# Hybrid layer on one core: split weights made three products ahead, and an index search that pauses for the sums of h

## The chip, the cores and the metric

The kernel runs on 1 core of one Trainium2 chip. The metric is device time in microseconds (us): 1913.03 us, median of 3 runs. The core has a matrix engine (TensorE, PE in the profile; its weight loads are the rows PEld), VectorE (DVE), ScalarE (ACT), GpSimd (POOL), and SyncE (SP), which here issues the DMA transfers. Every engine works through its own instructions in the order of the program; they meet through semaphores.

## The reference, cut to what matters

One decoder layer over 1024 tokens and 1024 channels, batch 1, all float32:

```
h    = rmsnorm(x) * (1 + scale1) + shift1            # from the conditioning c
proj = h @ w_in                                      # 1024 x 7240
qa, ka, va, iq, ik, iw, qr, kr, vr, gr, ga, gb = split(proj)
score = sum over index heads of iw * relu(iq . ik)   # causal; keep the 256 largest of a row
att  = softmax attention of qa, ka, va over the kept keys
ret  = chunkwise retention of qr, kr, vr
y    = sigmoid(ga) * (att @ w_attn_proj) + sigmoid(gb) * ((silu(gr) * groupnorm(ret)) @ w_ret_proj)
x    = x + gate1 * (y @ w_out)
x    = x + gate2 * ((silu(h2 @ w_ffn_gate) * (h2 @ w_ffn_up)) @ w_ffn_down)     # h2: second norm of x
out  = rmsnorm(x)
```

## The kernel before

A float32 product is made of three matmuls on values split in two: `hi` (rounded) and `lo = x - hi`, as hi·hi, hi·lo and lo·hi. A weight is split by ACT (`split_block` L703, tile `whi`) and then by POOL (L704, tile `wlo`).

The columns gr, qa, ka, two blocks of gb, and ga, and later the two input matrices of the feed-forward, use Strassen's scheme in Winograd's form on 2 x 2 blocks: seven products (M1 to M7) in place of eight. One `Stream` makes 256 output channels for all 1024 tokens: it loads two raw blocks of weights (`open`, L717), forms the weight side of each product (`factor`: DVE subtractions L732 and L728 for M5, M6, M7 and M4, the plain block for M1, M2 and M3), splits it, and multiplies (`product`, L760, L762 and L764: 12 matmuls of 128x128 by 128x512). M1, M6, M7 and M4 add up in one PSUM bank (`mm`), M5 and M3 in another (`lg`), and M2 has one of its own. ACT copies partial results out of PSUM (L743), DVE adds to them (L746), and `use` finishes each of the four output blocks. The order of products is M1, M5, M6, M3, M7, M2, M4; output 12 is complete after M3, 22 after M7, 11 after M2, 21 after M4.

There are 13 streams in the gate stage, counted from 0: 0 to 3 gr (silu), 4 and 5 qa, 6 and 7 ka, 8 gb, 9 to 12 ga. For the four q and k streams `use` does more: it splits the finished output block like a weight (again L703 and L704, here `whi<-kept`, `whi<-sums` or `whi<-spare`) and stores it with six DMAs (L829, L831). The streams 0 and 1 are interleaved product by product, as are the last two.

The other side of a product is a split part of h, or one of four sums of parts (S1, S2, S4, S3: adds L588 and L590 and the `lo` of L596 on DVE, the `hi` of L595 on ACT), made just before stream 0 needs them. S1 serves M5, S2 M6, S4 M3, and S3 M7.

The index search (`select_all`) finds the 256th largest score of each row bit by bit: for every bit from 30 to 0, six counts on DVE (L449, one for each block of rows) and two small updates (L454, L467; L470 at bit 0), then one more pass of counts and a tail of 30 instructions (L475 to L479). It has a low priority, and a scheduler puts it between other DVE work. Attention, which starts at about 960 us, needs its result.

A scheduler sets the order on every engine from the order of the code, the priorities and its own estimate of times. The code calls `product` for one product after the other, and each call makes its own split weight first.

Of the kernel before, what the change touches and what calls it, by code (L numbers as in the profile page):

```python
# [19 lines left out]
P = 128  # L20
# [4 lines left out]
H = 512  # L25
# [18 lines left out]
def tile_hybrid_layer(ctx: ExitStack, tc: tile.TileContext, x, c, w_ada, b_ada, norm1_w, w_in,  # L44
# [20 lines left out]
    def f32(ap):  # L65
        return ap.bitcast(F32)
# [367 lines left out]
    def select_all():  # L434

        tc.cur_priority += LATE
        n = len(score)  # L440
        cand, rej = (early.tile([P, 8], I32, name=x)[:, :n] for x in ("cand", "rej"))
        cnt, need = (early.tile([P, 8], F32, name=x)[:, :n] for x in ("cnt", "need"))
        eq = early.tile([P, S], U8, name="eq")
        rank = early.tile([P, S], I16, name="rank")
        at = [cand.bitcast(F32)[:, j:j + 1] for j in range(n)]

        def count(op, thr):
            for j, sc in enumerate(score):
                ins = nc.vector.tensor_scalar(eq[:, :sc.shape[1]], sc, thr[j], None, op0=op, op1=ALU.add,  # L449
                                              accum_out=cnt[:, j:j + 1])  # L450
            return ins

        def rejected(value):
            nc.vector.tensor_scalar(rej, cnt, float(TOPK), float(value), op0=ALU.is_lt, op1=ALU.mult)  # L454


        for j, sc in enumerate(score):
            ins = nc.vector.tensor_scalar(eq[:, :sc.shape[1]], sc, 0.0, None, op0=ALU.is_ge, op1=ALU.add,
                                          accum_out=cnt[:, j:j + 1])
            tc.add_manual_dep(ins.ins, last_score[0].ins.name, NOSYNC, reason="scores first")  # L460
        rejected(-1)
        nc.vector.tensor_scalar(cand, rej, 1 << 30, None, op0=ALU.bitwise_xor)
        for bit in range(30, -1, -1):
            count(ALU.is_ge, at)
            rejected(1 << bit)
            if bit:
                nc.vector.scalar_tensor_tensor(cand, cand, 1 << (bit - 1), rej, op0=ALU.bitwise_xor,  # L467
                                               op1=ALU.bitwise_xor)
            else:
                nc.vector.tensor_tensor(cand, cand, rej, op=ALU.bitwise_xor)  # L470
        count(ALU.is_gt, at)
        nc.vector.tensor_scalar(need, cnt, -1.0, float(TOPK), op0=ALU.mult, op1=ALU.add)
        for j, sc in enumerate(score):
            e, r = eq[:, :sc.shape[1]], rank[:, :sc.shape[1]]
            nc.vector.tensor_scalar(e, sc, at[j], None, op0=ALU.is_equal)  # L475
# [3 lines left out]
            nc.vector.scalar_tensor_tensor(sc, e, NEG, sc, op0=ALU.mult, op1=ALU.add)  # L479
        tc.cur_priority -= LATE  # L480
# [112 lines left out]
    def split_sum(to, k, src):  # L593
        hi, lo = (x[:, k, :] for x in side[to])
        nc.scalar.activation(hi, src, AF.Copy)  # L595
        nc.vector.tensor_sub(lo, src, f32(hi))  # L596

    mgen = mod_work()
    for hp in range(2):
# [106 lines left out]
    class Stream:  # L706


        def __init__(self, env, w, c0):
            self.env, self.w, self.c0 = env, w, c0  # L710
            self.c, self.ready = {}, {}

        def open(self):
            self.blocks = {}
            for kh in range(2):
                raw = self.env.raw().rearrange("p (k n) -> p k n", k=4)
                nc.sync.dma_start(out=raw, in_=self.w[kh * H:(kh + 1) * H, self.c0:self.c0 + 2 * P]  # L717
                                  .rearrange("(k p) n -> p k n", p=P))
# [28 lines left out]

        def product(self, m, after=None):

            early = m in self.ready  # L750
            whi, wlo = self.ready[m] if early else self.factor(m)
            hhi, hlo = self.env.side[SIDE[m]]
            if m == "M1":
                self.A = self.env.a()
# [20 lines left out]
                self.add("12", ps)  # L775
            if m == "M7":
                self.add("22", ps)
            if m == "M2" and early and self.env.late_m2:
# [8 lines left out]
    def ring_pair():  # L787
        return tuple(ring.tile([P, H], R, name=n, tag=n, bufs=RING) for n in ("whi", "wlo"))

    class GateEnv:  # L790
        late_m2 = False
        n_q, n_raw = 0, 0

        def __init__(self):
# [13 lines left out]
        def quad(self, *_):  # L808
            self.n_q += 1
            return quads[(self.n_q - 1) % len(quads)]  # L810

        def use(self, st, c):
            src = st.A if c == "21" else st.c[c]
            to = self.quad() if c == "21" else src
            hf, nt = int(c[0]) - 1, int(c[1]) - 1
            cs = slice(hf * H, (hf + 1) * H)
            if st.func is not None:
                nc.scalar.activation(to, src, st.func)
                nc.sync.dma_start(out=st.dst[nt][:, cs], in_=to)
                return  # L820

            if c == "21":
                nc.scalar.activation(to, src, AF.Copy)
            parts = ring_pair()
            split_block(to, *parts)
            which, dst = st.dst
            for e in range(2):
                h = 2 * (st.nt + nt) + e
                nc.sync.dma_start(out=rot_d[:, which, h, :, cs], in_=to[64 * e:64 * e + 16])  # L829
                for i, part in enumerate(parts):  # L830
                    nc.sync.dma_start(out=dst[h, 16:64, i, cs], in_=f32(part[64 * e + 16:64 * e + 64]))  # L831

# [32 lines left out]
    for to, terms in (("S1", [("h12", 1), ("h22", 1)]), ("S2", [(None, 1), ("h11", -1)]),  # L865
                      ("S4", [(None, -1), ("h21", 1)]), ("S3", [("h11", 1), ("h12", -1)])):
        for k in range(4):
            add_up(sums[k], [(n, k, sign) for n, sign in terms])
            split_sum(to, k, sums[k])
    for m in ORDER:  # L870
        for st in flow[:2]:
            st.product(m)


    def rope_load(hf):
# [37 lines left out]
        nc.scalar.activation(hi, sg, AF.Copy)  # L913
        nc.vector.tensor_sub(gT.lo[hf][:, k, :], sg, f32(hi))

    flow[2].open()
    rope = {}
    for n in range(2, len(flow) - 2):
        flow[n + 1].open()
        for m in ORDER:  # L920
            flow[n].product(m)
# [5 lines left out]
    flow[-1].open()  # L927
    for m in EARLY:
        for st in flow[-2:]:
            st.product(m)  # L930
    gT.alloc(0)
    k = 0
    staged = {}
    for m in ("M5", "M6", "M7", "M4", "M3"):
        if m == "M3":
            gT.alloc(1)
        for st in flow[-2:]:
            st.product(m)
            if k < KT:
                make_g(k, 0, *g_load(k, 0, *(f32(x) for x in ring_pair())))  # L940
            k += 1
        if m in ("M5", "M6"):
            stage = sp.tile([P, 8, H], F32, name="stage", tag={"M5": "S1", "M6": "S2"}[m])
            for i in range(4):
                staged[len(staged)] = g_load(len(staged), 1, stage[:, 2 * i, :], stage[:, 2 * i + 1, :])


    stacks = {}
# [344 lines left out]
        return ffn.tile([P, H], F32, name="tmp", tag="tmp", bufs=4)  # L1293

    class FfnEnv:
        late_m2 = True
# [98 lines left out]
    for p in range(NP):  # L1395
        for u, w in enumerate((w_ffn_gate, w_ffn_up)):
            st = streams[p, u] = Stream(fenv, w, 2 * p * P)
            st.p, st.u = p, u
            st.ready = {m: early_w[p, u, m] for m in EARLY if (p, u, m) in early_w}
    turns = {(0, 0, "M1"): {0: 6}, (0, 1, "M1"): {2: 7}}  # L1400
    for p in range(2):
        for m in EARLY:
# [18 lines left out]
    for m in ORDER:  # L1421
        if m not in EARLY:
            for st in flow[:2]:
                st.product(m)
                if m == "M4":
                    fenv.use(st, "11")
    for n in range(2, len(flow)):
        st = flow[n]
        if n == 2:
            st.open()  # L1430
        if n + 1 < len(flow):
            flow[n + 1].open()
        for m in ORDER:
            if st.p > 1 or m not in EARLY:
                st.product(m)
                if m == "M4" and st.p == 1:
                    fenv.use(st, "11")
                for task in todo[:2]:
                    task()
                del todo[:2]  # L1440
    def drain_todo():
        for task in todo:
            task()
# [180 lines left out]
```

## Time and profile before

| | |
|---|---|
| median of 3 runs (1912.8 to 1917.15) | 1913.03 us |
| the profiled execution, its own time | 1912.54 us |
| its span, first to last instruction | 1910.8 us |
| PE busy | 1749.4 us, 92% |
| DVE / POOL / ACT busy | 1210.5 / 930.6 / 741.3 us |
| mean granted PE clock | 0.958 |
| gate stage, first to last product | 499 to 874 us |
| feed-forward, products of gate and up | some 1250 to 1690 us |

The profiled execution stands 0.5 us below the median of the runs. A row of the timeline reads: start, duration, engine, source line, operation, output<-inputs, shapes, count, and in brackets the engine's idle time before it and what ended it. A row of a window reads: stretch, its length, then for each engine the busy time and (number of instructions), the granted PE clock (1.00 is full), the DMA engines' share, GB/s. A row of the waits reads: who waited for whom, us in total, times, longest. A busy PE is not PE at full pace: a matmul that runs at half the clock counts as busy.

### The profile page before, as it was taken

The numbers are of one execution on the slowest core, as the hardware profiler recorded it, in microseconds if no ns is written. First come the engines' busy times: TensorE is split into PE (matmuls) and PEld (weight loads), VectorE is DVE, ScalarE is ACT, GpSimd is POOL, SyncE is SP. The second block draws the span as 40 slices with busy tenths as digits, with TensorE's granted clock in tenths as the row PEclk, the third lists the DMA queues.
The fourth block names the chain that finished last, engine by engine and source line by source line (L and its number), as shares of the span: only waits on it lengthen the run. The fifth ranks groups of instructions, "written<-read, shape, count | busy, mean of one in ns | idle before, by whom it ended". The sixth has DMA issues, their size and how long they took to land. (4 is left out here: it accounts for less than half of the span.)

```text
span 1910.8 us, 24627 instructions
## 1 busy us (share of the span) xinstructions
PE 1749.4 (92%) x8266; PEld 1418.9 (74%) x8266; DVE 1210.5 (63%) x2088; ACT 741.3 (39%) x1448; POOL 930.6 (49%) x902
## 2 busy tenths in 40 slices
PE   5899999999888676999989999979998999999998
PEld 4788768787766454778867788858776788888887
DVE  7637699998999511544156564685666554567465
ACT  3426533323442112443057624553332333355444
POOL 4561393855541333953045462455444544466464
PEclk9999999999998667999999999989999999999999
DMA  8430353425321222577494361023676533277653
GB/s 287 144 89 26 108 150 132 155 53 155 91 94 59 61 81 71 168 243 211 148 205 116 122 232 44 22 77 100 230 254 215 171 105 99 83 242 245 197 171 121
DMA packets 184703, 266.49 MB, mean 139 GB/s; under 512 B 13872, under 2 KB 113664, under 8 KB 182144
## 3 DMA queue, kind: packets, MB, share of 16 engines
q1 hardware_dynamic: 184576, 264.91, 44.3%
q8 instruction: 65, 1.06, 0.2%
q14 instruction: 62, 0.51, 0.1%
HBM read 195.39 MB, written 69.47 MB: 139 GB/s over the span
## 5 line engine op out<-in xcount | busy, mean ns | idle before, releaser
L704 POOL TENSOR_TENSOR flo<-tmp,fhi 128x512 fp32r<-128x512 f32 x88 | 131.1, 1491 | 152.5 <-ACT fhi L703 130.7
L78 POOL TENSOR_TENSOR wlo<-wraw,whi 128x512 fp32r<-128x512 f32 (+2 forms) x116 | 142.9, 1245 | 101.1 <-ACT whi L77 96.0
L449 DVE TENSOR_SCALAR_CACHE_REDUCE eq<-score,cand 128x384 uint8<-128x384 f32 (+2 forms) x192 | 180.5, 940 | 3.6
L116 PE MATMUL mm<-whi,hT_hi 128*128 128x512 f32 (+1 forms) x432 | 162.6, 379 | 2.3 <-ACT qk L608 1.8
L119 PE MATMUL mm<-whi,hT_lo 128*128 128x512 f32 (+1 forms) x432 | 163.0, 379 | 0.0
L118 PE MATMUL mm<-wlo,hT_hi 128*128 128x512 f32 (+1 forms) x432 | 162.6, 377 | 0.0
L760 PE MATMUL ya<-hc,fhi 128*128 128x512 f32 x336 | 133.7, 399 | 13.5 <-DVE c L746 11.7
L762 PE MATMUL ya<-hc,fhi 128*128 128x512 f32 x336 | 132.7, 395 | 5.2 <-DVE hc L1390 5.2
L1472 DVE TENSOR_TENSOR dslot<-draw,dslot 128x512 fp32r<-128x512 f32 x88 | 92.2, 1075 | 70.3 <-ACT dslot L1471 64.1
L764 PE MATMUL ya<-hc,flo 128*128 128x512 f32 x336 | 131.2, 394 | 0.0
L1471 ACT ACTIVATE dslot<-draw 128x512 fp32r<-128x512 f32 x154 | 90.3, 626 | 97.5 <-PE ya L1490 36.2
L1472 POOL TENSOR_TENSOR dslot<-draw,dslot 128x512 fp32r<-128x512 f32 x66 | 97.4, 1485 | 62.1 <-ACT dslot L1471 61.8
L77 ACT ACTIVATE whi<-wraw 128x512 fp32r<-128x512 f32 (+2 forms) x116 | 67.0, 590 | 135.5 <-DMA wraw<-in_w_in_dram 55.8
L704 POOL TENSOR_TENSOR flo<-raws,fhi 128x512 fp32r<-128x512 f32 x58 | 81.6, 1408 | 72.1 <-ACT fhi L703 55.3
L760 PE MATMUL yb<-hc,fhi 128*128 128x512 f32 x248 | 98.0, 395 | 5.2 <-ACT hc L1389 3.7
L703 ACT ACTIVATE fhi<-tmp 128x512 fp32r<-128x512 f32 x88 | 55.3, 631 | 116.7 <-PE ya L762 71.7
L764 PE MATMUL yb<-hc,flo 128*128 128x512 f32 x248 | 96.8, 391 | 3.7 <-POOL flo L704 3.7
L762 PE MATMUL yb<-hc,fhi 128*128 128x512 f32 x248 | 96.8, 390 | 1.8 <-DVE hc L1390 1.7
L704 POOL TENSOR_TENSOR wlo<-wraw,whi 128x512 fp32r<-128x512 f32 x52 | 74.9, 1449 | 44.0 <-ACT whi L703 26.5
L1035 POOL TENSOR_SCALAR sx<-sx,mx 128x1024 f32<-128x1024 f32 (+7 forms) x64 | 47.6, 751 | 97.5 <-DVE mx L1034 72.4
L760 PE MATMUL mm<-hT_hi,whi 128*128 128x512 f32 x156 | 70.1, 453 | 26.4 <-ACT whi L703 25.4
L116 PEld LDWEIGHTS mm<-whi,hT_hi 128*128 128x128 f32 x432 | 82.1, 190 | 14.1 <-ACT qk L608 2.2
(400 smaller groups left out, 5016.3 us busy)
## 6 DMA issues: line engine op xcount, KB each, us to landing
draw<-act_d SPq DMA_DIRECT2D x77, 256.0 KB
mw<-in_w_ada_dram SPq DMA_DIRECT2D x32, 512.0 KB
act_d<-c SPq DMA_DIRECT2D x62, 256.0 KB
raw<-in_w_in_dram SPq DMA_DIRECT2D x26, 512.0 KB
raws<-in_w_ffn_gate_dram SPq DMA_DIRECT2D x24, 512.0 KB
raws<-in_w_ffn_up_dram SPq DMA_DIRECT2D x24, 512.0 KB
dw<-in_w_ffn_down_dram SPq DMA_DIRECT2D x22, 512.0 KB
dw_d<-dw SPq DMA_DIRECT2D x11, 1024.0 KB
```

The source lines that it names most:

```text
L77: nc.scalar.activation(hi[:, :n], raw[:, :n], AF.Copy)
L78: nc.gpsimd.tensor_sub(lo[:, :n], raw[:, :n], f32(hi[:, :n]))
L116: ins = nc.tensor.matmul(ps, lhsT=ahi, rhs=whi[:, :n], start=(i == 0), stop=False)
L118: nc.tensor.matmul(ps, lhsT=ahi, rhs=wlo[:, :n], start=False, stop=False)
L119: nc.tensor.matmul(ps, lhsT=alo, rhs=whi[:, :n], start=False, stop=(i == last))
L449: ins = nc.vector.tensor_scalar(eq[:, :sc.shape[1]], sc, thr[j], None, op0=op, op1=ALU.add, accum_out=cnt[:, j:j + 1])
L704: nc.gpsimd.tensor_sub(lo, src, f32(hi))
L760: mm = nc.tensor.matmul(ps, lhsT=whi[:, k, :], rhs=hhi[:, k, :], start=first, stop=False, skip_group_check=True)
L762: nc.tensor.matmul(ps, lhsT=whi[:, k, :], rhs=hlo[:, k, :], start=False, stop=False, skip_group_check=True)
L764: nc.tensor.matmul(ps, lhsT=wlo[:, k, :], rhs=hhi[:, k, :], start=False, stop=last, skip_group_check=True)
L1471: nc.scalar.activation(slot[:, 0], raw, AF.Copy)
L1472: lo_eng.tensor_sub(slot[:, 1], raw, f32(slot[:, 0]))
```

## The change

A `run` loop takes the list of products in their order and makes the split weight of a later product (three ahead in the gate stage, two in the feed-forward) before it calls `product` for the present one. `open` may now be called by `prepare`. A stream's output stores stay behind the loads of the next stream's raw weights in the DMA queue. The first count of bit 8 of the index search is put behind the last split of S3. Nothing is computed that was not computed before; the number of instructions on each engine is the same.

```diff
+    PAUSE = 8
+    paused = []
...
         for bit in range(30, -1, -1):
-            count(ALU.is_ge, at)
+            first = count(ALU.is_ge, at)
+            if bit == PAUSE:
+                paused.append(first)
...
+        def prepare(self, m):
+            if m not in self.ready:
+                self.open()
+                self.ready[m] = self.factor(m)
...
         def product(self, m, after=None):
-            early = m in self.ready
-            whi, wlo = self.ready[m] if early else self.factor(m)
+            self.prepare(m)
+            whi, wlo = self.ready[m]
...
+    def run(seq, ahead, then=lambda i: None):
+        for st, m in seq[:ahead]:
+            st.prepare(m)
+        for i, (st, m) in enumerate(seq):
+            if i + ahead < len(seq):
+                nxt, nm = seq[i + ahead]
+                nxt.prepare(nm)
+            st.product(m)
+            then(i)
...
+        def store(self, st, dst, src):
+            ins = nc.sync.dma_start(out=dst, in_=src)
+            if st.next:
+                turns_after(ins, st.next.loaded)
...
-            split_sum(to, k, sums[k])
-    for m in ORDER:
-        for st in flow[:2]:
-            st.product(m)
+            split = split_sum(to, k, sums[k])
+    turns_after(paused[0], split)
...
+    seq = [(st, m) for m in ORDER for st in flow[:2]]
+    seq += [(st, m) for st in flow[2:-2] for m in ORDER]
+    n_mid = len(seq)
+    seq += [(st, m) for m in ("M1", "M2", "M5", "M6", "M7", "M4", "M3") for st in flow[-2:]]
...
+    run(seq, 3, behind)
...
+    seq = [(st, m) for m in ORDER if m not in EARLY for st in flow[:2]]
+    seq += [(st, m) for st in flow[2:] for m in ORDER if not (st.early and m in EARLY)]
...
+    run(seq, 2, behind)
```

Lines move a little: L703 is L706 in the changed kernel, L743 L754, L746 L757, L823 L850, L728 L739, L732 L743, L449 L450, L596 L599.

Three places show what the scheduler makes of it. The first is ACT from the copy of output 21 of one q stream (`kept<-mm`, L823) into the next one; `whi<-raw` and `whi<-wraw` are weights, `whi<-kept` and `whi<-spare` split output blocks. Before:

```order
L823 ACTIVATE kept<-mm 128x512
L703 ACTIVATE whi<-kept 128x512
L703 ACTIVATE whi<-raw_4910 128x512
L703 ACTIVATE whi<-wraw 128x512 x2
L703 ACTIVATE whi<-raw_4907 128x512
L743 ACTIVATE kept<-mm 128x512
L743 ACTIVATE kept<-lg 128x512
L743 ACTIVATE spare<-mm 128x512
L703 ACTIVATE whi<-spare 128x512
L703 ACTIVATE whi<-wraw 128x512
L703 ACTIVATE whi<-kept 128x512
L703 ACTIVATE whi<-raw_4907 128x512
```

Behind the split of output 21 stand the weights of M1, M5, M6 and M3, and then, one behind each later output block, those of M7, M2, M4 and the next stream's M1. The same place in the changed kernel:

```order
L850 ACTIVATE kept<-mm 128x512
L706 ACTIVATE whi<-kept 128x512
L706 ACTIVATE whi<-raw_4907 128x512
L706 ACTIVATE whi<-wraw 128x512
L706 ACTIVATE whi<-raw_4907 128x512
L754 ACTIVATE kept<-lg 128x512
L706 ACTIVATE whi<-wraw 128x512
L754 ACTIVATE spare<-mm 128x512
L706 ACTIVATE whi<-spare 128x512
L706 ACTIVATE whi<-raw_4908 128x512
L706 ACTIVATE whi<-kept 128x512
L706 ACTIVATE whi<-wraw 128x512
```

Behind output 21 now stand M3, M7 and M2 and then M4; behind output 12 (`spare`) stands M1 of the next stream, three products on. POOL's order moves in the same way.

The second place is DVE at the end of the sums; `hT_lo` is the `lo` half of S3, which takes the place of a part of h, and the rows `eq,cnt` are counts of the search. Before:

```order
L596 TENSOR_TENSOR hT_lo_122<-sums,hT_hi_121 128x512
L449 TENSOR_SCALAR eq,cnt<-score_769,cand 128x512
L596 TENSOR_TENSOR hT_lo_122<-sums,hT_hi_121 128x512
L732 TENSOR_TENSOR wraw<-raw_4908 128x512
L449 TENSOR_SCALAR eq,cnt<-score_770,cand 128x640
L728 TENSOR_TENSOR wraw<-raw_4907,wraw 128x512
L746 TENSOR_TENSOR sums<-sums,lg 128x512
L449 TENSOR_SCALAR eq,cnt<-score_771,cand 128x768
```

After:

```order
L599 TENSOR_TENSOR hT_lo_122<-sums,hT_hi_121 128x512
L743 TENSOR_TENSOR wraw<-raw_4907,wraw 128x512
L757 TENSOR_TENSOR kept<-kept,lg 128x512
L599 TENSOR_TENSOR hT_lo_122<-sums,hT_hi_121 128x512
L450 TENSOR_SCALAR eq,cnt<-score_768,cand 128x384
L450 TENSOR_SCALAR eq,cnt<-score_769,cand 128x512
L450 TENSOR_SCALAR eq,cnt<-score_770,cand 128x640
L450 TENSOR_SCALAR eq,cnt<-score_771,cand 128x768
```

No count stands among the sums any more; the counts in the first list are those of bit 4, the first after S3 in the second list those of bit 8. From there on DVE has the same work of the streams as before, with the last nine bits and the tail between it: the tail ends after the 21st add of the streams (the last add of stream 6), where it ended after the 15th (the last of stream 4).

The third place is the feed-forward. There no row moves: from the first instruction of attention to the end the order on PE, DVE, ACT, POOL and SP is, line numbers apart, the same before and after.

More of the change, by code (lines that the diff above doesn't have):

```diff
@@ L447, in count @@
         def count(op, thr):
[L448 to L451, printed above, removed]
+            ins = [nc.vector.tensor_scalar(eq[:, :sc.shape[1]], sc, thr[j], None, op0=op, op1=ALU.add,
+                                           accum_out=cnt[:, j:j + 1]) for j, sc in enumerate(score)]
+            return ins[0]
         def rejected(value):
@@ L595, in split_sum @@
         nc.scalar.activation(hi, src, AF.Copy)
-        nc.vector.tensor_sub(lo, src, f32(hi))
+        return nc.vector.tensor_sub(lo, src, f32(hi))
     mgen = mod_work()
@@ L710, in __init__ @@
             self.env, self.w, self.c0 = env, w, c0
-            self.c, self.ready = {}, {}
+            self.c, self.ready, self.blocks = {}, {}, {}
+            self.early = False
+            self.next = None
         def open(self):
-            self.blocks = {}
+            if self.blocks:
+                return
             for kh in range(2):
                 raw = self.env.raw().rearrange("p (k n) -> p k n", k=4)
-                nc.sync.dma_start(out=raw, in_=self.w[kh * H:(kh + 1) * H, self.c0:self.c0 + 2 * P]
-                                  .rearrange("(k p) n -> p k n", p=P))
+                self.loaded = nc.sync.dma_start(out=raw, in_=self.w[kh * H:(kh + 1) * H, self.c0:self.c0 + 2 * P]
+                                                .rearrange("(k p) n -> p k n", p=P))
                 for f in range(2):
                     self.blocks[f"{kh + 1}{f + 1}"] = raw[:, :, f * P:(f + 1) * P]
+        def prepare(self, m):
+            if m not in self.ready:
+                self.open()
+                self.ready[m] = self.factor(m)
         def factor(self, m):
@@ L818, in use @@
                 nc.scalar.activation(to, src, st.func)
-                nc.sync.dma_start(out=st.dst[nt][:, cs], in_=to)
+                self.store(st, st.dst[nt][:, cs], to)
                 return
@@ L828, in use @@
                 h = 2 * (st.nt + nt) + e
-                nc.sync.dma_start(out=rot_d[:, which, h, :, cs], in_=to[64 * e:64 * e + 16])
+                self.store(st, rot_d[:, which, h, :, cs], to[64 * e:64 * e + 16])
                 for i, part in enumerate(parts):
@@ L914, in make_g, with behind @@
         nc.vector.tensor_sub(gT.lo[hf][:, k, :], sg, f32(hi))
[L916 to L921, printed above, removed]
+    seq = [(st, m) for m in ORDER for st in flow[:2]]
+    seq += [(st, m) for st in flow[2:-2] for m in ORDER]
+    n_mid = len(seq)
+    seq += [(st, m) for m in ("M1", "M2", "M5", "M6", "M7", "M4", "M3") for st in flow[-2:]]
+    rope, staged = {}, {}
+    def behind(i):
+        n, m = 2 + (i - 14) // 7, seq[i][1]
+        if 14 <= i < n_mid:
+            if m == "M1":
+                flow[n + 1].open()
+                flow[n].next = flow[n + 1]
             if n in (8, 9) and m == "M1":
@@ L925, in tile_hybrid_layer @@
                 rope_store(n - 9, *rope[n - 9])
[L927 to L935, printed above, removed]
-            gT.alloc(1)
[L937 to L945, printed above, removed]
+        if i == n_mid:
+            flow[-1].open()
+        k = i - n_mid - 4
+        if k == -1:
+            gT.alloc(0)
+        if 0 <= k < KT:
+            make_g(k, 0, *g_load(k, 0, *(f32(x) for x in ring_pair())))
+            if k in (1, 3):
+                stage = sp.tile([P, 8, H], F32, name="stage", tag=f"S{(k + 1) // 2}")
+                for i in range(4):
+                    staged[len(staged)] = g_load(len(staged), 1, stage[:, 2 * i, :], stage[:, 2 * i + 1, :])
+        if k == KT - 1:
+            gT.alloc(1)
+    run(seq, 3, behind)
     stacks = {}
@@ L1420, in tile_hybrid_layer, with behind @@
     flow[1].open()
[L1421 to L1431, printed above, removed]
-            flow[n + 1].open()
[L1433 to L1440, printed above, removed]
+    seq = [(st, m) for m in ORDER if m not in EARLY for st in flow[:2]]
+    seq += [(st, m) for st in flow[2:] for m in ORDER if not (st.early and m in EARLY)]
+    def behind(i):
+        st, m = seq[i]
+        if st.early and m == "M4":
+            fenv.use(st, "11")
+        if i < 10:
+            return
+        n = flow.index(st)
+        if seq[i - 1][0] is not st and n + 1 < len(flow):
+            flow[n + 1].open()
+        for task in todo[:2]:
+            task()
+        del todo[:2]
+    run(seq, 2, behind)
     def drain_todo():
```

5 lines of the change are left out of this document (2 added, 3 removed).

## The prediction

> **What bounds the kernel now.** I read the page first, for where PE leaves its full pace, then the stretches there, the waits, and the timeline of one stall.
>
> ```profile
> span 1910.8 us, 24627 instructions
> ...
> PE   5899999999888676999989999979998999999998
> ...
> PEclk9999999999998667999999999989999999999999
> ```
>
> The span in 40 slices of 47.8 us: PE is busy nearly everywhere, but in slices 14 to 16, some 620 to 770 us, it falls to 6 to 8 tenths and its clock to 6 or 7 tenths. That is where the q and k streams stand. The stretches cut at the products themselves:
>
> ```profile
> 499.00:607.00 108.00, 93.93 (x385) 74.89 (x384) 104.49 (x178) 39.68 (x69) 40.20 (x26) 0.94 0.28 88
> 607.00:767.00 160.00, 104.65 (x290) 71.63 (x289) 53.12 (x51) 30.89 (x55) 53.20 (x40) 0.70 0.23 66
> 767.00:874.00 107.00, 104.61 (x461) 85.27 (x462) 53.24 (x51) 47.80 (x85) 71.33 (x52) 0.97 0.72 229
> 775.00:825.00 50.00, 48.83 (x214) 39.78 (x213) 28.90 (x21) 22.96 (x41) 47.42 (x34) 1.00 0.58 186
> ```
>
> After the length come PE, PEld, DVE, ACT and POOL, each with its count. From 607 to 767 us PE did 290 matmuls in 160 us, while no other engine was busy for more than 54 of the 160. So this stretch is bound by a chain, not by an engine. Who waited there:
>
> ```profile
> PE mm L760 <- ACT whi L703: 25.4, 12, 3.3
> ...
> PE mm L764 <- POOL wlo L704: 13.1, 10, 2.5
> ...
> PE lg L760 <- ACT whi L703: 12.3, 4, 6.2
> ...
> PE lg L764 <- POOL wlo L704: 4.6, 4, 1.6
> ```
>
> Together 55.4 us, 16 times for a `whi` and 14 times for a `wlo`: four products in each of four streams. One of them, M7 of the second q stream behind its M3:
>
> ```profile
> 657.88 0.39 PE L762 MATMUL lg<-S,whi 128*128 128x512 f32 x1
> 658.11 0.39 PE L764 MATMUL lg<-S,wlo 128*128 128x512 f32 x1
> 658.61 0.69 DVE L746 TENSOR_TENSOR spare<-spare,lg 128x512 f32<-128x512 f32 x1 [8.48 <-PE lg L764]
> ...
> 659.38 0.63 ACT L703 ACTIVATE whi<-spare 128x512 fp32r<-128x512 f32 x1 [2.96 <-DVE spare L746]
> 659.91 0.61 ACT L703 ACTIVATE whi<-wraw 128x512 fp32r<-128x512 f32 x1
> 660.08 1.29 POOL L704 TENSOR_TENSOR wlo<-spare,whi 128x512 fp32r<-128x512 f32 x1 [10.51 <-ACT whi L703]
> 660.58 0.50 PE L760 MATMUL mm<-hT_hi,whi 128*128 128x512 f32 x1 [2.08 <-ACT whi L703]
> ...
> 661.32 1.27 POOL L704 TENSOR_TENSOR wlo<-wraw,whi 128x512 fp32r<-128x512 f32 x1
> ...
> 662.64 0.80 PE L764 MATMUL mm<-hT_hi,wlo 128*128 128x512 f32 x1 [1.33 <-POOL wlo L704]
> 663.24 0.63 PE L760 MATMUL mm<-hT_hi,whi 128*128 128x512 f32 x1
> 663.66 0.63 PE L762 MATMUL mm<-hT_lo,whi 128*128 128x512 f32 x1
> ...
> 666.65 0.63 PE L764 MATMUL mm<-hT_hi,wlo 128*128 128x512 f32 x1
> ```
>
> The weight of M7 (`wraw`) depends on nothing that is late. It stands on ACT and POOL behind the split of output 12 (`spare`), and that waits for M3, the product just finished. PE thus waits for its own last product by way of DVE, ACT and POOL: 2.08 and then 1.33 us. After it the matmuls start 0.42 us apart (663.24, 663.66) where they start 0.227 apart before it (657.88, 658.11). One product, 2.72 us at full pace (12 x 0.227), takes from 658.3 to 667.1.
>
> **The ceiling.** At 0.227 us the 385 matmuls of 499 to 607 need 87.3 of 108 us, 20.7 lost. The 290 of 607 to 767 need 65.7 of 160, 94.3 lost: 55.4 by the waits, the other 39 by the half pace behind them. From 767 to 874 stand 35 products (95.2) and some 5 us of transposes, 7 lost. In all 122 us, and no more can be won, since the order behind the gate stage does not move.
>
> **The change part by part.**
>
> The move of the weights. What a stream takes now shows in the copies of its output 21, and what SP does for one output and one load in SP's timeline:
>
> ```profile
> L823 ACT ACTIVATE kept<-mm x2: 597/598/598, 641.5 to 726.0; 128x512 f32<-128x512 f32 x2
> L823 ACT ACTIVATE sums<-mm x1: 597/597/597, 684.5 to 684.5; 128x512 f32<-128x512 f32 x1
> L823 ACT ACTIVATE spare<-mm x1: 597/597/597, 765.1 to 765.1; 128x512 f32<-128x512 f32 x1
> ...
> 668.03 1.20 SPq L829 DMA_DIRECT2D rot_d<-kept  x2
> 669.33 0.82 SPq L831 DMA_DIRECT2D q_d<-whi  x2
> ...
> 671.32 0.39 SPq L717 DMA_DIRECT2D raw<-in_w_in_dram  x1
> ```
>
> The copies (least, median and greatest ns, then first and last start) are 39 to 43 us apart. Behind output 12 of stream n now stands M1 of stream n+1, with M7, M2 and M4 between: 8.2 us of PE. By the rows above its `whi` is ready 2.2 us and its `wlo` 4.3 us after M3 ends (658.3 to 662.6). The others have the same 3 products in hand. POOL needs, for each q or k stream, 7 weights and 4 outputs at 1.28, 14.1 us; ACT 11 splits and 4 copies at 0.6, 9 us; PE 84 x 0.227 = 19.1 us. So PE should become the bound of these streams. That POOL can be nearly full while PE is at pace shows in the fourth stretch above: POOL 47.4 of 50 us, 214 matmuls (the pace allows 220). Term: up to -94.3.
>
> SP. A stream issues 2 loads and per output 6 stores, some 12 us by these rows (4 x (1.2 + 2 x 0.82) + 2 x 0.39); the stores now stand behind the next stream's loads, which need buffers that are free since M4 of the stream before was split. Cost nothing, hidden under 19 us of PE; without that cover ACT would wait for free tiles (rival 3).
>
> The sums of h. DVE is full while they are made, and counts stand among them:
>
> ```profile
> 490.00:555.40 65.40, 51.33 (x198) 39.84 (x197) 65.33 (x92) 30.03 (x53) 36.55 (x23) 0.90 0.28 83
> ...
> 490.00:555.40 65.40, 11.67 (x26) 0.90 0.28 83
> ```
>
> The second row is L449 alone; with the small updates, two of them slow, the search took some 14.4 of 65.3 us. Without it S3, whose last `lo` ends at 555.4 (the row at 554.49 below), is ready near 490 + 51 = 541. PE can do twelve products until then (all of streams 0 and 1 but M7 and M4, and two of stream 2: 32.7 us from 499), so of its 20.7 us some 10 stay. Term: -11, ends 0 (PE waits for something else) and -20.7.
>
> The search moves behind the sums, and this is the price. Its times:
>
> ```profile
> 472.39 0.60 DVE L449 TENSOR_SCALAR_CACHE_REDUCE eq<-score,cand 128x384 uint8<-128x384 f32 x1
> ...
> 554.49 1.00 DVE L596 TENSOR_TENSOR hT_lo<-sums,hT_hi 128x512 fp32r<-128x512 f32 x1
> ...
> 584.01 0.61 DVE L449 TENSOR_SCALAR_CACHE_REDUCE eq<-score,cand 128x384 uint8<-128x384 f32 x1
> ...
> 590.35 0.61 DVE L449 TENSOR_SCALAR_CACHE_REDUCE eq<-score,cand 128x384 uint8<-128x384 f32 x1
> ...
> 604.14 0.41 DVE L475 TENSOR_SCALAR eq<-score,cand 128x384 uint8<-128x384 f32 x1
> ...
> 638.08 1.23 DVE L479 SCALAR_TENSOR_TENSOR score<-eq,score 128x1024 f32<-128x1024 uint8 x1
> ```
>
> A pass alone takes 6.34 us (584.01 to 590.35, bit 1). Bit 8 began at 472.39; bits 8 to 5 and two counts of bit 4, 26.7 us, ran before S3 was done, partly in time that DVE had free. Now nine bits and a last pass, 10 x 6.3, and the tail (604.14 to 639.3, less 4 others of 0.6: 33) come behind 541: 96 us. Between them stand 18 adds and 17 subtractions of the streams:
>
> ```profile
> 566.39 1.75 DVE L732 TENSOR_TENSOR wraw<-raw,wraw 128x512 f32<-128x512 f32 x1
> ...
> 567.55 1.74 POOL L704 TENSOR_TENSOR wlo<-wraw,whi 128x512 fp32r<-128x512 f32 x1
> ...
> 568.73 0.68 DVE L746 TENSOR_TENSOR kept<-kept,lg 128x512 f32<-128x512 f32 x1
> ```
>
> An add reads PSUM and costs 0.6 from start to start. A subtraction reads SBUF twice and takes 0.68 alone, 1.75 beside POOL. 18 x 0.6 = 11 and 17 x (0.6 to 1.7) = 10 to 29, of which I take 20, since POOL will be busy for half to three quarters of the time. DVE so reaches the tail's end at 541 + 96 + 31 = 668, and the 21st add, some 8 us earlier in its order, at 660 (649 to 672 with the ends and slower tail rows). At that add PE has done 48 products. At pace, with the 10 us that stay, this is 499 + 131 + 10 = 640. So DVE, not PE, should set the pace until the search ends, and takes back 20 us (0 to 32). A place for a rule: PE's short waits that remain. The Trainium skill (TensorE: Matmul & The Clock Gate, HAM oscillation) says that only gaps over some 3.4 us throttle PE, so that such waits would leave the clock alone. The rows above speak against it here: 2.08 and 1.33 us, with two matmuls between, are followed by half pace. I go by the rows; since DVE sets the time there, the half pace is inside the 20.
>
> From 660 there remain 43 products (117 us), 5 of transposes, and some 4 lost where 7 were: the stage ends near 786, not at 874. That is -88, or by terms -94 - 11 - 3 + 20.
>
> The feed-forward part of `run` costs and brings nothing: no row of its order moves, so its waits stay as they are. Attention needs the scores at some 870; the search is done by 680.
>
> Sum, against the profiled execution: 1912.5 - 88 = 1824.5. The median of the runs is 0.5 us above it, which is nothing here: I say 1825. A measurement of this kernel tells some 0.3% (6 us) from no change.
>
> **The rivals.**
>
> 1. DVE is the bound by much more. All 17 subtractions at 1.7 (29 us), and the tail's two-input rows slowed as well (up to 15 us more), and streams 7 to 12 still short of `wlo` by a few us each: the stage ends 20 to 45 us later than I say, 1845 to 1870. For it speak the 1.75 us row above and DVE's 104.5 of 108 us in the first stretch. Against it: in that stretch, from 560 to 607, PE ran at pace with the search beside it. The Trainium skill (SBUF — State Buffer, two separate sides) has the pair of ports that DVE and POOL share as an exclusive lock, which blocks the loser for a whole instruction. By it alone each of 41 such operations could wait for a 1.28 us one, 52 us; the trace bears out 1.07 for one, and only where they meet.
>
> 2. Everything fits: DVE keeps pace and the stage loses next to nothing. Then some 112 to 118 of the 122 us come back: 1795 to 1801. Against it stands the work of 96 + 31 us on DVE in a time in which PE needs 100.
>
> 3. Slower: tiles run out. A q or k stream takes 11 pairs of split tiles, as many as the ring has, so each is given again one stream later, and an output's pair is free only when its stores have landed. ACT, in order, would stand at an output's split with all weights behind it. A stream has four outputs; to eat the gain, each of the 16 would have to wait 6 us, so that a stream takes some 43 us again. No wait of ACT for a store stands in this trace, where a stream takes 39 to 43; at 19 the stores have half the time. It would give 1915 to 1930.
>
> 4. The reorder does less than it says: output splits still stand before the weight that PE needs, for a cause not in the order (a raw block that lands late, a copy out of PSUM). Two of four stalls of 6 us stay: 4 x 12 = 48 back, 1872, or up to 1905.
>
> **Chances and range.** My forecast, 1803 to 1845, has 0.60. Rival 1 has 0.20, since its price is the least known; rival 2 has 0.10, rival 4 has 0.07, rival 3 has 0.03. The forecast's own ends are the bounds of the terms: -88 with 0 to 32 in place of 20, and a few us for the sums. The range reaches into rivals 1 and 2: 1798 to 1860, which leaves out most of rivals 3 and 4, and the outer parts of 1 and 2, together some 0.18. Faster by over 0.3%: 0.95; within: 0.02; slower: 0.03.
>
> **What the profile after would show.** Products of the gate stage from 499 to near 786. PE's waits for `whi` and `wlo` in the q and k streams gone, or a few us; the copies of output 21 some 20 to 27 us apart, not 39 to 43. S3's last `lo` near 541; the tail of the search ending between 655 and 685, and until then DVE full and PE's remaining waits ending on DVE. POOL some three quarters busy in the q and k streams. The feed-forward and all behind the gate stage as long as before. Wrong I would be if PE waits for `wlo` because POOL is slowed more than I take, if SP or the loads hold ACT, or if the stage behind the gates, where DMA is full around 850 to 920, gives some of it back.

## The result, and the profile after

The changed kernel takes 1836.20 us (median of 4 runs, 1831.56 to 1837.94) against 1913.38 of the kernel before: a ratio of 0.9589, 95% interval 0.9567 to 0.9610. It is 77 us faster; 1825 was forecast, with 1798 to 1860 as the range.

The page after, the span in 40 slices (45.9 us each):

```profile
span 1834.9 us, 24613 instructions
...
PE   5899989999989979999989999889998999999998
...
PEclk9999999999989999999989999999999999999999
```

The trough is nearly gone: PE falls to 7 tenths in one slice (642 to 688 us), and its granted clock stands at 9 in all slices but two, where it is 8. The stretches of the gate stage (columns as before: length, then PE, PEld, DVE, ACT and POOL busy with counts, granted clock, DMA share, GB/s):

```profile
499.00:541.00 42.00, 33.16 (x117) 25.02 (x117) 40.81 (x51) 18.57 (x33) 22.51 (x13) 0.84 0.26 76
541.00:599.00 58.00, 58.00 (x256) 47.74 (x256) 56.65 (x116) 22.28 (x40) 22.14 (x17) 1.00 0.36 118
599.00:700.00 101.00, 84.30 (x351) 65.84 (x350) 89.51 (x106) 37.09 (x66) 69.74 (x45) 0.97 0.40 114
700.00:790.00 90.00, 87.61 (x399) 71.50 (x398) 44.01 (x43) 37.90 (x68) 59.62 (x43) 1.00 0.76 243
```

At 0.227 us a matmul the four stretches need 26.6, 58.1, 79.7 and 90.6 us. So 15.4 us are lost in the sums of h, nothing until 599, 21.3 from 599 to 700, nothing behind: 37 in all. The gate stage ran from 499.0 to 871.9 us before (372.9); now it runs from 497.7 to 790.3 (292.6). It has 1125 matmuls in both, which need 255.4 us at this pace, so by the same count 117.5 us were lost before. The prediction's 122 counts the stage up to 874 and its transposes at some 5 us.

The waits from 599 to 700 (who waited for whom: us, times, longest):

```profile
ACT whi L706 <- DVE sums L757: 18.9, 3, 9.0
ACT whi L706 <- DVE wraw L739: 15.4, 3, 8.3
ACT whi L706 <- DVE kept L757: 12.2, 4, 5.0
...
PE mm L775 <- POOL wlo L707: 5.2, 3, 2.3
PE lg L771 <- ACT sums L754: 5.0, 1, 5.0
```

PE's waits for `whi` and `wlo` were 55.4 us from 607 to 767 before; here they are 8.7 (with three groups of 2.1 and less that are not shown). Who is late now stands in the first three rows: ACT waits for adds (L757) and subtractions (L739) of DVE.

The marks that the prediction named: the copies of output 21, the last `lo` of S3 (L599), and the last rows of the search's tail (L482):

```profile
L850 ACT ACTIVATE kept<-mm x2: 598/599/600, 613.3 to 666.6; 128x512 f32<-128x512 f32 x2
L850 ACT ACTIVATE sums<-mm x1: 578/578/578, 634.9 to 634.9; 128x512 f32<-128x512 f32 x1
L850 ACT ACTIVATE spare<-mm x1: 598/598/598, 688.6 to 688.6; 128x512 f32<-128x512 f32 x1
...
L599 DVE TENSOR_TENSOR hT_lo<-sums,hT_hi x4: 678/934/1778, 535.8 to 544.6; 128x512 fp32r<-128x512 f32 x4
...
L482 DVE SCALAR_TENSOR_TENSOR score<-eq,score x6: 547/1015/2299, 633.7 to 674.9; 128x384 f32<-128x384 uint8 x1, 128x512 f32<-128x512 uint8 x1, 128x640 f32<-128x640 uint8 x1, 128x768 f32<-128x768 uint8 x1
```

The copies are 21.6, 31.7 and 22.0 us apart (39 to 43 before, 20 to 27 forecast; the long one is the time beside the tail); S3 is done at 545 (541 forecast, 555 before); the tail ends at 677 (668 forecast).

### The profile page after: what moved, and what is told of

The parts are those of the page before. It is cut to its first block, busy times and chain, and to the rows that moved or that the text cites. A ratio compares the mean times of both kernels' runs of the same rounds, so it can differ in the third digit from the quotient of the medians.

```text
span 1834.9 us, 24613 instructions
## 1 busy us (share of the span) xinstructions
PE 1712.6 (93%) x8266; PEld 1399.1 (76%) x8266; DVE 1222.0 (67%) x2088; ACT 739.8 (40%) x1448; POOL 937.4 (51%) x902
## 5 line engine op out<-in xcount | busy, mean ns | idle before, releaser
L450 DVE TENSOR_SCALAR_CACHE_REDUCE eq<-score,cand 128x384 uint8<-128x384 f32 (+2 forms) x192 | 180.7, 941 | 4.2
L706 ACT ACTIVATE fhi<-tmp 128x512 fp32r<-128x512 f32 x88 | 55.3, 632 | 117.4 <-PE ya L773 72.7
L707 POOL TENSOR_TENSOR wlo<-wraw,whi 128x512 fp32r<-128x512 f32 x52 | 83.6, 1615 | 30.9 <-ACT whi L706 25.1
L119 PEld LDWEIGHTS mm<-whi,hT_lo 128*128 128x128 f32 x432 | 82.3, 191 | 12.7
```

The source lines that it names most:

```text
L119: nc.tensor.matmul(ps, lhsT=alo, rhs=whi[:, :n], start=False, stop=(i == last))
L450: ins = [nc.vector.tensor_scalar(eq[:, :sc.shape[1]], sc, thr[j], None, op0=op, op1=ALU.add, accum_out=cnt[:, j:j + 1]) for j, sc in enume ...
L707: nc.gpsimd.tensor_sub(lo, src, f32(hi))
```

## The experiments

Two theories stood at first. One, from the prediction: the moved weights bring nearly all, and DVE, with the search behind the sums, is the bound until the search ends. The other: the pause brings a good part itself, or what is lost from 599 to 700 has nothing to do with the search. The table gives for each kernel the time, the gate stage in its profiled execution, and the time lost in it by stretches (length less 0.227 us for each matmul, in us; the last stretch runs to the stage's end). "Ahead" is how many products ahead a weight is made in the gate stage, 3 where nothing is said; in the kernel before and with the pause only it is none.

| kernel | median us | gate stage | 499-545 | 545-600 | 600-680 | 680-end | behind the stage |
|---|---|---|---|---|---|---|---|
| before | 1913.4 | 372.9 | 16 | 5 | 48 | 49 | 1038.9 |
| changed | 1836.2 | 292.6 | 15 | 0 | 21 | 0 | 1044.6 |
| ahead only | 1829.3 | 291.5 | 16 | 4 | 16 | 0 | 1037.9 |
| pause only | 1914.9 | 376.8 | 15 | 1 | 53 | 51 | 1036.3 |
| pause at bit 6 | 1835.1 | 295.1 | 13 | 3 | 21 | 2 | 1035.2 |
| tail behind stream 7 | 1833.9 | 296.0 | 15 | 0 | 1 | 23 | 1039.6 |
| 1 ahead | 1843.4 | 303.2 | 15 | 0 | 29 | 2 | 1037.2 |
| 2 ahead | 1837.1 | 296.6 | 16 | 0 | 26 | 0 | 1039.5 |
| no pause, tail behind the stage | 1828.8 | 276.6 | 16 | 4 | 0 | 1 | 1050.6 |
| ACT in POOL's place | 1795.4 | 255.3 | 0 | 0 | 2 | 0 | 1038.9 |
| no pause, tail spread | 1824.4 | 285.3 | 17 | 2 | 0 | 10 | 1039.9 |
| pause at 6, tail spread | 1821.5 | 283.1 | 14 | 1 | 2 | 9 | 1039.5 |
| POOL writes zeros | 1796.1 | 257.7 | 0 | 0 | 4 | 0 | 1039.3 |
| feed-forward 0 ahead | 1830.8 | 294.9 | 15 | 0 | 21 | 2 | 1037.1 |

**One part of the change alone.** The weights without the pause:

```diff
-    turns_after(paused[0], split)
```

> Weights three products ahead, but the search does not pause: the counts of bits 8 to 5 stand among the sums of h as before. Theory (until the 21st add of the streams DVE sets the end of the gate stage, and the pause left DVE unused for some 12 us between 470 and 490): the sums end near 555 again and PE loses some 20 us there, but DVE has done 12 us more of its work, so the 21st add comes 10 to 12 us earlier: 1822 to 1830 us, faster than the changed kernel. Rival (the early sums are worth what they save PE, about 5 to 11 us, and nothing behind takes it back): 1840 to 1847 us.

1829.3 us, 0.9576 of the kernel before (0.9549 to 0.9603). The time is what the theory said, but not for its reason: the gate stage is only 1 us shorter than with the pause. The tail ended 28 us earlier (its last row began at 646.8, not at 674.9), and yet PE lost 16 us beside it, where it had lost 21. The rest of the 7 us lies behind the gate stage, where no order differs. The 21st add, which was to come 10 to 12 us earlier, ended at 666.5, where it ended at 663.5 in the changed kernel.

The pause without the weights:

```diff
-    run(seq, 3, behind)
+    run(seq, 0, behind)
```

> The search pauses, but in the gate stage every product's weight is split just before its product, as before (ahead 0). Theory (the move of the weights is worth nearly all): the 4 stalls of each q and k stream are back, PE's waits for whi and wlo at 40 to 55 us, copies of output 21 again 39 to 43 us apart, 1895 to 1910 us. Rival (the pause brings a good part of the gain, since the search no longer stands in the streams' way): 1840 to 1880 us.

1914.9 us, a ratio of 1.0019 (1.0006 to 1.0031): no gain at all, and a little above what was expected. The waits from 600 to 780 of this run:

```profile
PE mm L771 <- ACT whi L706: 36.8, 12, 10.9
PE mm L775 <- POOL wlo L707: 12.4, 11, 2.0
```

with 8.6 and 4.8 more for `lg`. All four stalls of each stream are back. So the whole of the gain is the move of the weights; the rival is out.

**Where the search stands.** More bits before the pause, in time that DVE had free, and the last pass and tail moved behind the q and k streams:

```diff
-    PAUSE = 8
+    PAUSE = 6
```

> As the changed kernel, but the pause is at bit 6 in place of 8, so that two more bits (12.6 us of DVE) run between 470 and 490, where DVE was 5.2 and 2.4 of 10 us busy. Theory (DVE sets the end until the search's tail): tail and 21st add 10 to 12 us earlier, 1823 to 1829 us. Rival (what is lost from 599 to 681 is lost to POOL and DVE slowing each other in the q and k streams, not to the search): 1834 to 1838 us.

1835.1 us (0.9597, 0.9574 to 0.9620): a miss. The tail's last row began at 663.4, 11.5 us earlier, and the stretch from 600 to 680 still lost 21 us. The edit did more than its one line says: the scheduler also put the tail ahead of three adds more (it ended behind the 18th add of the streams, not the 21st), so the 21st add ended at 668.8, 5 us later than in the changed kernel.

```diff
-        count(ALU.is_gt, at)
+        paused.append(count(ALU.is_gt, at))
...
     run(seq, 3, behind)
+    turns_after(paused[1], flow[7].added)     # added: the stream's last DVE add
```

> As the changed kernel, but the last pass of counts and the tail of the search stand behind the last DVE add of stream 7. Theory (DVE sets the end): some 45 us of search leave DVE's order ahead of the adds of streams 5 and 6, so PE keeps its pace there; of the 21 us lost from 599 to 700 some 15 to 20 come back, the tail now runs beside streams 8 to 10, where DVE was 54% busy: 1816 to 1823 us. Rival (the tail then delays the subtractions of streams 8 to 12 and takes it back there): 1830 to 1840 us. If POOL and DVE slow each other the tail's scans will again show 2.5 to 3.3 us, since POOL is busy there too.

1833.9 us (0.9595, 0.9568 to 0.9622), as the rival had it. Two stretches and two waits from 665 to 793 of this run:

```profile
600.00:680.00 80.00, 78.54 (x346) 64.34 (x345) 52.99 (x75) 34.75 (x62) 61.88 (x45) 1.00 0.49 143
680.00:793.10 113.10, 93.64 (x399) 75.45 (x398) 78.18 (x73) 40.56 (x71) 67.11 (x43) 0.89 0.62 196
```

```profile
PE mm L771 <- DVE kept L757: 8.6, 1, 8.6
PE mm L771 <- DVE sums L757: 7.7, 1, 7.7
```

The q and k streams run at full pace (346 matmuls in 80 us) once no tail stands among them, so it was the search that held them. But the loss moved along with the tail: of streams 8 to 12 the add at 696.4 stands on DVE behind four tail rows and the one at 732.3 behind three, and PE waits for the banks that they empty. So the amount of DVE's work up to the 21st add does not give the loss by itself. In the changed kernel DVE was 54% busy where the tail went (32.4 of 60 us from 680 to 740), and the loss was the same. What costs, in these orders, is the tail as one piece ahead of the adds.

**How many products ahead.**

```diff
-    run(seq, 3, behind)
+    run(seq, 1, behind)      # and 2 in another kernel
```

> As the changed kernel, but in the gate stage the weight of only the next product is made ahead (1 in place of 3). Theory (a weight must stand ahead of the product whose output split it would wait behind): M7's weight now stands ahead of output 12, but M2's stands behind it. Output 12's split takes POOL until 4.3 us after M3 ends, M7 covers 2.7, so each of the 16 outputs leaves PE waiting some 1.5 to 3 us, with half clock behind it: 1855 to 1880 us. Rival (any order that takes the weight from behind the output is enough): 1832 to 1840 us.

> As the changed kernel, but 2 products ahead in the gate stage. Theory: two products, 5.4 us, cover the 4.3 us of an output's split, so this is as good as three: 1832 to 1842 us. Rival (POOL, slowed by DVE to 1.7 us an operation, needs the third product): 1845 to 1860 us.

With 2 it takes 1837.1 us (0.9609, 0.9595 to 0.9624), the same as 3. With 1 it takes 1843.4 (0.9642, 0.9622 to 0.9662), between what the theory and its rival had: PE's waits for `whi` and `wlo` from 600 to 720 are 22 us (9 with 3), but a part of them stands in time that the tail took anyway. Most of the gain (70 of 77 us) needs only that the next weight no longer stands behind the output just made.

**The tail where POOL is quiet.** No pause, the tail behind the last DVE add of the gate stage (`paused[1]` and `added` as above):

```diff
-    turns_after(paused[0], split)
...
     run(seq, 3, behind)
+    turns_after(paused[1], flow[-1].added)
```

> Weights three ahead, no pause, and the last pass of counts and the tail of the search behind the last DVE add of the gate stage, where POOL is little used (17 of 68 us) and the products that follow don't wait for DVE adds. Theory (DVE and its tail are what PE waits for after 600 us, wherever the tail stands among the streams): no loss from 600 to the gate stage's end, which comes near 775 in place of 789.5; attention, at some 870, still finds the scores done: 1813 to 1820 us. Rival (the tail then holds up what DVE does for the retention product and attention): 1826 to 1840 us.

The gate stage does what the theory said: it ends at 775.5, and its stretch from 600 to 680 has 352 matmuls in 80 us. The time is the rival's, 1828.8 us (0.9567, 0.9553 to 0.9581), since the tail (785 to 832) then stands ahead of DVE's work for the retention product, and what follows the stage takes 1050.6 us, some 11 more than elsewhere:

```profile
PE mm L129 <- DVE sgr L988: 5.8, 1, 5.8
PE mm L131 <- DVE gT_lo L938: 2.8, 2, 2.3
```

**POOL beside DVE.** Here the subtraction that makes `lo` is left out in the gate stage. In one kernel ACT writes a plain copy in its place, in the other POOL writes zeros:

```diff
+            if self.env is genv:
+                nc.scalar.activation(hi, src, AF.Copy)
+                nc.scalar.activation(lo, src, AF.Copy)      # the other: nc.gpsimd.memset(f32(lo), 0.0)
+                return hi, lo
             split_block(src, hi, lo)
...
-            split_block(to, *parts)                         # the output blocks likewise
```

> As the changed kernel, but in the gate stage ACT writes a second plain copy into the lo half in place of POOL's subtraction (the subtraction is left out), so POOL does nothing beside DVE there. Theory (DVE's rows that read SBUF twice are slowed by POOL's splits, and that is a good part of DVE's price): DVE's subtractions and sums take 0.68 each, not 0.7 to 1.78, S3 is done near 537 in place of 545, the tail's 30 rows take some 33 us in place of 42, and the gate stage ends 15 to 25 us earlier: 1810 to 1822 us. Rival (the slow rows do not matter, PE waits for the order): 1828 us or more.

> As the changed kernel, but in the gate stage POOL fills the lo half with zeros, reading nothing from SBUF (the subtraction is left out). POOL stays in the chain of every weight, with an instruction of its own. Theory (what slows DVE is POOL reading SBUF beside it): DVE's rows take 0.68 again and the stage is nearly as short as with ACT in POOL's place, 1793 to 1806 us. Rival (POOL's place in the chain is what costs, however DVE's rows run): 1815 us or more. If writing alone is enough to slow DVE, its rows stay at 0.7 to 1.7.

1795.4 (0.9382, 0.9356 to 0.9407) and 1796.1 us (0.9399, 0.9385 to 0.9414): 40 us less than the changed kernel, with pause and tail left as they are there, and more than the 14 to 26 that were expected of the first. The whole gate stage with ACT in POOL's place, with POOL writing zeros, and of the changed kernel:

```profile
499.10:754.40 255.30, 252.99 (x1125) 207.43 (x1124) 178.02 (x310) 165.73 (x306) 21.13 (x15) 1.00 0.54 169
```

```profile
502.60:760.30 257.70, 253.59 (x1125) 208.90 (x1124) 177.47 (x308) 115.89 (x204) 70.29 (x112) 0.99 0.54 169
```

```profile
497.70:790.30 292.60, 264.67 (x1125) 211.46 (x1124) 232.28 (x314) 116.13 (x205) 175.31 (x116) 0.97 0.48 149
```

For about the same 310 instructions DVE is busy for 178 us in place of 232. The same groups on DVE, first of the changed kernel (540 to 675), then with POOL writing zeros (499 to 670, so with more subtractions):

```profile
L450 DVE TENSOR_SCALAR_CACHE_REDUCE eq<-score,cand 128x384 uint8<-128x384 f32 (+5 forms) x60 | 56.6, 943 | 1.6
L479 DVE TENSOR_TENSOR_SCAN rank<-eq 128x384 int16<-128x384 uint8 (+5 forms) x6 | 13.1, 2186 | 0.2
...
L481 DVE TENSOR_SCALAR score<-score,cand 128x384 f32<-128x384 f32 (+5 forms) x6 | 7.3, 1209 | 0.0
...
L743 DVE TENSOR_TENSOR wraw<-raw 128x512 f32<-128x512 f32 x5 | 7.2, 1449 | 0.0
```

```profile
L450 DVE TENSOR_SCALAR_CACHE_REDUCE eq<-score,cand 128x384 uint8<-128x384 f32 (+5 forms) x60 | 56.6, 944 | 1.5
L479 DVE TENSOR_TENSOR_SCAN rank<-eq 128x384 int16<-128x384 uint8 (+5 forms) x6 | 9.7, 1620 | 0.1
...
L743 DVE TENSOR_TENSOR wraw<-raw 128x512 f32<-128x512 f32 x9 | 6.2, 686 | 1.6 <-ACT whi L750 1.6
...
L481 DVE TENSOR_SCALAR score<-score,cand 128x384 f32<-128x384 f32 (+5 forms) x6 | 3.8, 625 | 0.0
```

The counts (L450) are as long in both; on the mean the subtractions and the tail's rows take up to twice as long beside a POOL that reads. With that gone, the tail in one piece among the streams costs 4 us or less, and the sums cost none.

One thing stays open. POOL's fill takes 0.53 us where its subtraction takes 1.28 or more, and it does not wait for `whi`: its waits are for buffers that PE or a store still holds. So POOL's part of the chain of each weight is gone in both kernels, other than the second expectation has it, and no run divides the 40 us between this and DVE's rows. In the sums the waits point to DVE: of PE's 8.7 us of waits from 497 to 541, 5.4 are for the `lo` of a sum on DVE, the others for ACT, none for POOL. Beside the tail PE's own waits for `wlo` were 5.6 us, and where PE lost most, DVE was full and POOL was not (two stretches of the changed kernel):

```profile
641.00:651.00 10.00, 4.97 (x14) 3.77 (x13) 9.90 (x10) 1.60 (x3) 5.88 (x4) 0.66 0.47 130
651.00:661.00 10.00, 7.58 (x33) 5.60 (x32) 9.93 (x10) 1.15 (x2) 2.88 (x2) 1.00 0.16 49
```

So it is likely, but not shown by itself, that the tail costs what it does because its rows are long beside POOL.

**A kernel that uses it.** The 30 tail rows put one by one behind the subtractions and adds of streams 8 to 12, without a pause and with one at bit 6 (the lines that collect `tail` and `side_ops` are left out; the index comes to `i`):

```diff
     run(seq, 3, behind)
+    gaps = [ins for st, ins in side_ops if st in flow[8:]]
+    for i, ins in enumerate(tail):
+        turns_after(ins, gaps[i * 1 // 1])
```

> Weights three ahead, no pause, and the 30 rows of the search's tail put one by one behind the DVE subtractions and adds of streams 8 to 12. Theory (the tail costs what stands behind it in one piece; one row between two of the streams' is covered by three products in hand): PE loses some 20 us in the sums and next to nothing from 600 to the gate stage's end, which comes at 773 to 778, and unlike the tail behind the gate stage this holds nothing up there: 1811 to 1818 us. Rival (the rows, slowed beside POOL, make the weights of streams 8 to 12 late wherever they stand): 1825 to 1832 us.

> As the kernel with the spread tail, but with the pause at bit 6. Theory (with the tail out of the way a pause is worth something, since DVE has slack behind the sums): S3 done near 546 in place of 555, PE loses some 12 us there in place of 20 and nothing behind: 1803 to 1812 us. Rival (the bits that were held back make DVE late behind the sums again): as the spread tail without a pause or up to 8 us more.

1824.4 us (0.9541, 0.9528 to 0.9554) and 1821.5 us (0.9531, 0.9516 to 0.9546). Both are above what was expected, since from 680 on some 10 us are still lost (what takes them is not shown), and their intervals overlap, so the pause is again worth nothing that shows. The second is faster than the changed kernel (0.9567 to 0.9610) by intervals that do not meet. The two are the fastest of the kernels here that leave nothing out.

**The feed-forward.**

```diff
-    run(seq, 2, behind)
+    run(seq, 0, behind)
```

> As the changed kernel, but in the feed-forward no weight is made ahead in the code (0 in place of 2). The order on every engine is the same as in the changed kernel. Theory (this part of the change does nothing, and the 474 to 481 us that the feed-forward took in the runs so far are the same program's own spread): 1830 to 1838 us, gate stage 291 to 296 us. Rival (it does cost something, so the feed-forward falls to 474 to 476 here and the time to 1828 to 1832).

1830.8 us (0.9576, 0.9563 to 0.9589), which lies in the range of the theory and of its rival. What decides is the order: it is the same on every engine as in the changed kernel, from the first instruction to the last. The gate stage is 2 us longer than there and the part behind it 7.5 shorter. The feed-forward's `ya` products before, in the changed kernel, and here:

```profile
L760 PE MATMUL ya<-hc,fhi x336: 387/389/796, 1255.2 to 1701.2; 128*128 128x512 f32 x168
```

```profile
L771 PE MATMUL ya<-hc,fhi x336: 388/389/796, 1174.7 to 1624.8; 128*128 128x512 f32 x168
```

```profile
L771 PE MATMUL ya<-hc,fhi x336: 389/389/796, 1176.6 to 1619.8; 128*128 128x512 f32 x168
```

446.0, 450.1 and 443.2 us; with the pause at 6, which has 2 ahead in the feed-forward, they took 442.9. All have one order there, so some 7 us are the spread of this part from one execution to another (1035 to 1045 us behind the stage in all kernels but the one that put the tail there). A difference between two single profiles is read from the gate stage, not from the span.

## Why the prediction was nearly right, step by step

- **The weights, -94: right.** Each part alone shows that they bring the whole gain, and with the tail out of their way (behind stream 7, or behind the gate stage) the q and k streams run at full pace. Most of it needs one product ahead; two and three are the same.
- **The sums, -11: measured -5.** S3 came at 545, not 541, and 15.4 us were lost, not 10. The term took the search out of DVE's time and left the other rows as long as before. But most of these rows read SBUF twice, and beside POOL's splits of the weights they take up to 1.78 us; with POOL's splits gone nothing is lost there.
- **The price of the search, +20: measured 21.** For this one order the sum holds: the 21st add ended at 663.5 (660 forecast), when PE had begun 49 products (48) and lost 32 us of the gate stage (30). It holds partly by luck: S3 came 4 us late and the tail's 30 rows took 42 us, not 33 (28 with POOL writing zeros), while the rest took some 4 less than I summed. And it is not a price of the search in other orders, as the runs with the pause at 6 and with the tail moved show: PE loses 11 to 23 us wherever the tail stands in one piece ahead of something that PE needs, and about 10 with the tail spread out.
- **The pause as a whole.** The terms -11 and +20 did not say what the pause itself does, as they mixed its gain with the cost that the search has anyway. Measured, it does nothing that these runs can tell: 1829.3 without it, 1836.2 and 1830.8 with it, with intervals that overlap.
- **The late streams, -3: right, from two wrong numbers.** Up to the stage's end at 871.9, and by the count of the table, 2.3 us were lost there before (452 matmuls in 104.9 us), not 7; behind 700 none can be seen now, where I left 4.
- **The feed-forward, 0: right,** but its own spread was not in the sum. Of the 12 us between the forecast span (1822.8) and the measured one, 4 lie in the gate stage (790.3, not 786), 6 behind it, mostly in the feed-forward, and 2 in reading the stage's end before as 874 where it is 871.9.
- **The rival of the ports** was given 0.20. Its mechanism is seen, its time (1845 to 1870) did not come. The Trainium skill (SBUF — State Buffer, two separate sides) has the ports that DVE and POOL share as a lock held for a whole instruction. The runs agree with the rule, as the rows of the last section show. By it I worked out 52 us for 41 operations and gave it little weight, since one row bore out only 1.07 us. DVE's excess in the gate stage is 54 us (232 less 178), some 50 for rows that both kernels have there. That this is near 52 is chance: the 50 are of all rows, the sums too, which I had not counted, and the changed kernel is 40 us slower for it at most.
- **The clock.** I set two waits of 2.08 and 1.33 us, with half pace behind them, against the rule of the Trainium skill (TensorE: Matmul & The Clock Gate, HAM oscillation) that only gaps over some 3.4 us throttle. In the trace after, the wait of 5.03 us below is followed by starts 0.42 us apart for 4.0 us, the waits of 0.71 and 1.71 by none, which fits the rule. But the clock fell inside the wait: the granted clock of 0.66 from 641 to 651, shown above, stands for 6.8 us at half, and 4.0 of them lie behind the wait, so it fell some 2.3 us after the last matmul ended, sooner than 3.4. In the kernel before it fell at 661.6, inside the second of the two waits (the last two rows below), so the first one and some 0.3 us of the second were enough there. What exactly sets it stays open; a pair of waits was not tried by itself.

```profile
640.89 0.39 PE L775 MATMUL mm<-S,wlo 128*128 128x512 f32 x1
646.31 0.80 PE L771 MATMUL lg<-S,whi 128*128 128x512 f32 x1 [5.03 <-ACT sums L754]
646.90 0.63 PE L773 MATMUL lg<-S,whi 128*128 128x512 f32 x1
647.32 0.63 PE L775 MATMUL lg<-S,wlo 128*128 128x512 f32 x1
...
650.31 0.47 PE L771 MATMUL lg<-S,whi 128*128 128x512 f32 x1
650.62 0.39 PE L773 MATMUL lg<-S,whi 128*128 128x512 f32 x1
...
656.97 0.50 PE L771 MATMUL mm<-hT_hi,whi 128*128 128x512 f32 x1 [0.71 <-ACT whi L706]
657.31 0.40 PE L773 MATMUL mm<-hT_lo,whi 128*128 128x512 f32 x1
659.41 0.50 PE L775 MATMUL mm<-hT_hi,wlo 128*128 128x512 f32 x1 [1.71 <-POOL wlo L707]
659.75 0.39 PE L771 MATMUL mm<-hT_hi,whi 128*128 128x512 f32 x1
```

```profile
655.00:661.60 6.60, 4.24 (x18) 2.87 (x16) 0.69 (x1) 1.75 (x3) 1.52 (x2) 1.00 0.04 11
661.60:675.30 13.70, 9.80 (x21) 6.78 (x22) 1.38 (x2) 1.15 (x2) 3.49 (x3) 0.50 0.34 100
```

## What to carry to other kernels

Where PE waits for its own last product by way of other engines, look for work that depends on nothing late but stands behind work that does; one product of lead brought most of the gain here. Work that fills an engine which goes in program order is costed by the piece that stands ahead of something needed soon, not by its sum alone: here 11 to 23 us in one piece, about 10 spread out. And DVE and POOL are costed together where both read SBUF: the same DVE rows took up to twice as long on the mean beside POOL's splits.

## What the runs showed of the hardware that was not expected

In the stretch below DVE and POOL do not share by slowing each other evenly, they take turns. These are the two engines at the end of the tail in the changed kernel (rows of both by time):

```profile
670.53 1.70 POOL L707 TENSOR_TENSOR wlo<-wraw,whi 128x512 fp32r<-128x512 f32 x1
...
671.03 2.28 DVE L480 SCALAR_TENSOR_TENSOR eq<-rank,need,eq 128x1024 uint8<-128x1024 int16 x1
...
672.19 2.27 POOL L707 TENSOR_TENSOR wlo<-kept,whi 128x512 fp32r<-128x512 f32 x1
...
673.23 1.78 DVE L743 TENSOR_TENSOR wraw<-raw 128x512 f32<-128x512 f32 x1
...
674.42 1.73 POOL L707 TENSOR_TENSOR wlo<-raw,whi 128x512 fp32r<-128x512 f32 x1
```

L480 (1.28 us alone) begins at 671.03, POOL's row ends at 672.23, and L480 ends 1.08 us after that, at 673.31. POOL's next row (1.28 us alone) began at 672.19 and ends 1.15 us after L480 does, at 674.46; L743 (0.68 alone) ends 0.55 us after that, at 675.01. Each waits until the other's instruction has ended, and both show the wait as busy time. The counts with an accumulator (L450) are not slowed (0.943 and 0.944 us on the mean), and beside a fill by POOL, which reads nothing, DVE's subtractions stay at 0.69.
